# Left operands of the second MLP matmul loaded one product at a time into the shared tile pool, and every weight laid out in HBM as contiguous 512 KB blocks

## The chip, the cores and the metric

The kernel runs on one core of a Trainium2 chip. The metric is device microseconds from start to end of one execution. Engines are named as in the profile: PE (TensorE matmul), PEld (its weight load), DVE (VectorE), ACT (ScalarE), POOL (GpSimd), SP (SyncE, which here issues nearly all loads). "SPq" is SP's instruction queue. Each engine works through its own instructions in order, so a waiting instruction holds everything behind it on the same engine.

## The reference

One encoder layer in float32 for 512 tokens and a model width of 2048: neighbourhood attention, then a squared-ReLU MLP.

```
x = x + neighbourhood_attention(rms_norm(x, norm_mix), w_qkv, q_gain, k_gain, rel_bias, w_o)
a = relu(rms_norm(x, norm_mlp) @ w1)        # 512 x 2048 @ 2048 x 8192
x = x + (a * a) @ w2                        # 512 x 8192 @ 8192 x 2048
```

The change touches how weights reach the chip (all of them) and how `a * a`, written to HBM by the first MLP matmul, comes back as the left operand of the second.

## The kernel before, in words

**Precision.** Every float32 operand is split into a high part `h` (rounded to fp32r by ACT) and a low part `l` (the rest, by DVE). A product takes three matmuls: high x high, high x low, low x high.

**Stages.** First the units `v`, `q`, `k` (attention, heads run beside them), then `o`, all through `multiply` (L304). Then the MLP: eight units `h0` to `h7` for `w1` and eight units `y0_0` to `y3_1` for `w2` (block c of 2048 hidden columns, half p of the output), all objects of class `Pair` and run by `multiply_pair` (L250).

**A pair.** A pair multiplies 512 tokens by a 2048 x 1024 piece of a weight with seven products instead of eight (a Strassen-Winograd scheme). Products m = 1, 5, 6, 4 (`FIRST`) run for b = 0 to 3, then m = 2, 3, 7 (`SECOND`) for b = 0 to 3. One (m, b) is a *chunk*: one 256 x 512 weight quarter (512 KB) and 12 matmuls of 512 columns; a pair has 28 chunks, 336 matmuls. The right operands of products 5, 6, 4 and 7 are sums of quarters, built in a chain: DVE adds the raw quarter to the previous one (L219, four of seven chunks). Then ACT makes `wh` (L235) and DVE `wl` (L237).

**Pools and queue order.** Raw weights lie in the pool `raw`: ten buffers of 512 KB. `load_raw` (L189) issues the load of a chunk on SP six chunks or more ahead; it starts when a buffer of `raw` comes free, which is when DVE's `wl` of an older chunk is done. The split parts `wh`, `wl` have three buffers each. Nearly everything else (left operands, outputs on their way, temporaries) lies in the pool `tiles`, 70 buffers of 256 KB. A scheduler sets each engine's order at build time; the program does not reorder at run time.

**From h to y.** After a pair `h`, the squared result is transposed in *windows* (L702) and stored to HBM tensors `z_t` by POOL (L712, L713, L723): the four blocks and three sums of them that seven products need. Left operands of block c of the second matmul are loaded during the last pair that uses the block before (h7, y0_1, y1_1, y2_1; a *handover pair* below). `pass_on` (L753) does this: per b two loads after product 1 (`xa`, `xb`: products 5, 6 and 4, 1) and two after product 2 (`xa`: product 2; `xb`: products 3, 7), all into buffers of `raw`, that is four of its buffers per b. After product 4 (and 7) `split_left` splits them into high and low parts `a_z` (L556 on ACT, L558 on DVE) in `tiles`.

**Results.** The output of each pair y0 to y2 is added into HBM by POOL: eight accumulating DMAs of 256 KB (L750), all in the last chunks of the pair and just after. The pairs y3 load these sums (`ys`, L734), add, and store.

Of the kernel before, what the change touches and what calls it, by code (L numbers as in the profile page):

```python
# [44 lines left out]
class Unit:  # L45
# [4 lines left out]


    def __init__(self, name, src, act, done, kind):
        self.name, self.src, self.act, self.done, self.kind = name, src, act, done, kind
        self.n = KT // 4 if kind == "narrow" else KT
        self.raw, self.parts, self.ps = {}, {}, None
        self.load, self.before, self.after, self.lag = None, None, None, 0


class Pair:
# [27 lines left out]
    def quarter(self, m, b):  # L87
        r, c = self.QUARTER[m]
        r, c = self.row + (4 * b + 2 * r) * P, self.col + c * T
        return self.w[r:r + 2 * P, c:c + T].rearrange("(k p) n -> p k n", p=P)  # L90


@with_exitstack
def natten_mlp_kernel(ctx, tc, x_t, gains, w_qkv, bias, w_o, w1, w2, out_t):
    nc = tc.nc
# [75 lines left out]
    def later(lag, fn):  # L171
        side.append((pos[0] + lag, fn))
# [16 lines left out]
    def load_raw(u, i):  # L189
        if isinstance(u, Pair):  # L190
            t = u.raw[i] = raw.tile([P, 2, T], F32, tag="raw", name=f"w_{u.name}_{i[0]}")
            nc.sync.dma_start(out=t, in_=u.quarter(*i))
            return
        if i % 2:
            return
        t = raw.tile([P, 2, T], F32, tag="raw", name=f"w_{u.name}_{i}")
        if u.load is not None and i == 0:
            for m in range(2):
                nc.sync.dma_start(out=t[:, m], in_=u.src[m * P:(m + 1) * P])
                u.load(m)  # L200
# [552 lines left out]
    def pass_on(dst, block):  # L753

        loaded = {}

        loads = {1: ((T + HALF, 5, 6), (HALF, 4, 1)), 2: ((0, 2), (5 * HALF, 3, 7))}

        def split_left(b, stage):
            for (c, *ms), t in zip(loads[stage], loaded.pop((b, stage))):  # L760
                for i, m in enumerate(ms):
                    yield from parts_of(dst[b], m, t[:, :, i * HALF:(i + 1) * HALF], f"a{m}_z{block}_{b}")

        def after(m, b):
            if m in (1, 2):
                ts = []
                for i, (c, *ms) in enumerate(loads[m]):
                    t = two(f"{'xb' if i else 'xa'}_z{block}_{b}_{m}")
                    n = len(ms) * HALF
                    nc.sync.dma_start(out=t[:, :, :n],  # L770
                                      in_=z_t[4 * block + b][:, c:c + n].rearrange("(k p) n -> p k n", p=P))
                    ts.append(t)
                loaded[b, m] = ts
# [78 lines left out]
```

## Time and profile before

| | |
|---|---|
| median of 3 runs | 2107.44 us (2104.9 to 2107.91) |
| the profiled execution | 2108.97 us |
| its span, first to last instruction | 2107.2 us |
| PE busy, PEld busy | 2055.6 us (98%), 1691.3 us (80%) |
| DVE busy, ACT busy | 1546.3 us (73%), 1043.6 us (50%) |
| data moved by DMA | 400 MB, mean 190 GB/s |

A busy PE counts a matmul from start to modelled end, and matmuls overlap in the pipeline: one of 512 columns is listed with 0.39 us and the next starts 0.23 us later. So time that PE loses is read best from starts: how long a pair takes against 336 steps. The clock column is the granted TensorE clock as a share of full speed. A DMA's landing time runs from its issue on the queue to its completion.

### The profile page before, as it was taken

The numbers are of one execution on the slowest core, as the hardware profiler recorded it, in microseconds if no ns is written. First come the engines' busy times: TensorE is split into PE (matmuls) and PEld (weight loads), VectorE is DVE, ScalarE is ACT, GpSimd is POOL, SyncE is SP. The second block draws the span as 40 slices with busy tenths as digits, with TensorE's granted clock in tenths as the row PEclk, the third lists the DMA queues.
The fourth block names the chain that finished last, engine by engine and source line by source line (L and its number), as shares of the span: only waits on it lengthen the run. The fifth ranks groups of instructions, "written<-read, shape, count | busy, mean of one in ns | idle before, by whom it ended". The sixth has DMA issues, their size and how long they took to land.

```text
span 2107.2 us, 25091 instructions
## 1 busy us (share of the span) xinstructions
PE 2055.6 (98%) x9330; PEld 1691.3 (80%) x9330; DVE 1546.3 (73%) x1884; ACT 1043.6 (50%) x1412; POOL 103.7 (5%) x166
## 2 busy tenths in 40 slices
PE   9999999999999999999999999999998999989998
PEld 7888888888888887888888888887877777777777
DVE  6674774764774568778878877898797687779786
ACT  6663653654663444444544544564453445345333
POOL 0000000000000000010010110110201001011000
PEclk9999999999999999999999999999999999999999
DMA  9333333323233346676866866887888689589774
GB/s 285 100 91 90 97 90 94 96 85 101 94 100 130 102 151 217 180 223 185 276 217 205 272 209 210 289 275 256 257 305 246 193 255 274 197 239 273 257 234 147
DMA packets 251931, 400.14 MB, mean 190 GB/s; under 512 B 14240, under 2 KB 83872, under 8 KB 251808
## 3 DMA queue, kind: packets, MB, share of 16 engines
q1 hardware_dynamic: 234768, 352.37, 52.5%
q0 software_dynamic: 16896, 46.15, 7.7%
q8 instruction: 73, 1.20, 0.2%
q14 instruction: 50, 0.41, 0.1%
q10 hardware_dynamic: 144, 0.02, 0.0%
HBM read 348.14 MB, written 50.33 MB: 189 GB/s over the span
## 4 chain that ended last, share of the span: by engine, by line
PE 40%; issue 36%; DMA 12%; DVE 8%; POOL 3%; ACT 0%; SPq 0%; DVEq 0%; POOLq 0%; ACTq 0%
DMA w_y<-in_w 11%; PE mm_q L304 8%; PE mm_k L304 8%; PE mm_v L304 8%; PE mm_o L304 5%; DVE wl_y L237 4%; DVE w_y L219 2%; PE y_y L250 2%; PE x_y L250 2%; PE z_y L250 2%; PE w_y L250 1%; PE o L471 1%; POOL z L712 1%; POOL z L713 1%; POOL z L723 1%
## 5 line engine op out<-in xcount | busy, mean ns | idle before, releaser
L235 ACT ACTIVATE wh_y<-w_y 128x1024 fp32r<-128x1024 f32 x224 | 237.6, 1061 | 327.9 <-PE y_y L250 91.5
L235 ACT ACTIVATE wh_h<-w_h 128x1024 fp32r<-128x1024 f32 x224 | 237.6, 1061 | 287.0 <-PE y_h L250 85.5
L237 DVE TENSOR_TENSOR wl_h<-w_h,wh_h 128x1024 fp32r<-128x1024 f32 x224 | 272.7, 1221 | 73.9 <-ACT wh_h L235 73.4
L237 DVE TENSOR_TENSOR wl_y<-w_y,wh_y 128x1024 fp32r<-128x1024 f32 x224 | 270.8, 1219 | 24.4 <-ACT wh_y L235 24.3
L219 DVE TENSOR_TENSOR w_y<-w_y,w_y 128x1024 f32<-128x1024 f32 x128 | 156.4, 1222 | 112.5 <-DMA w_y<-in_w 110.9
L219 DVE TENSOR_TENSOR w_h<-w_h,w_h 128x1024 f32<-128x1024 f32 x128 | 155.2, 1220 | 50.9 <-DMA w_h<-in_w 50.6
L237 DVE TENSOR_TENSOR wl_o<-w_o,wh_o 128x1024 fp32r<-128x1024 f32 x32 | 39.1, 1223 | 58.5 <-ACT wh_o L235 58.4
L235 ACT ACTIVATE wh_o<-w_o 128x1024 fp32r<-128x1024 f32 x32 | 33.9, 1060 | 80.0 <-PE mm_o L304 66.2
L235 ACT ACTIVATE wh_q<-w_q 128x1024 fp32r<-128x1024 f32 x32 | 34.0, 1062 | 77.8 <-PE mm_q L304 30.2
L237 DVE TENSOR_TENSOR wl_q<-w_q,wh_q 128x1024 fp32r<-128x1024 f32 x32 | 39.2, 1226 | 43.6 <-ACT wh_q L235 42.1
L237 DVE TENSOR_TENSOR wl_k<-w_k,wh_k 128x1024 fp32r<-128x1024 f32 x32 | 39.1, 1223 | 37.8 <-ACT wh_k L235 37.8
L235 ACT ACTIVATE wh_k<-w_k 128x1024 fp32r<-128x1024 f32 x32 | 34.0, 1062 | 50.7 <-PE mm_q L304 31.1
L235 ACT ACTIVATE wh_v<-w_v 128x1024 fp32r<-128x1024 f32 x31 | 32.8, 1058 | 47.4 <-PE mm_v L304 23.4
L237 DVE TENSOR_TENSOR wl_v<-w_v,wh_v 128x1024 fp32r<-128x1024 f32 x31 | 37.9, 1224 | 23.0 <-ACT wh_v L235 22.6
L713 POOL DMA_DIRECT2D z<-zt x32 | 17.3, 542 | 467.3 <-ACT zt L708 467.0
L602 POOL DMA_DIRECT2D y<-x1t_0s x4 | 2.3, 586 | 770.9 <-ACT x1t_0s L601 770.9
L708 ACT ACTIVATE zt<-zt 128x512 f32<-128x512 f32 x64 | 37.1, 579 | 2.0 <-DVE a_z_1l L558 2.0
L511 ACT ACTIVATE t<-t,st 128x256 f32<-128x256 f32 x64 | 32.0, 501 | 10.6 <-DVE st L507 10.6
L250 PE MATMUL x_y<-wl_y,a_z_0h 128*128 128x512 f32 x64 | 26.2, 409 | 9.8 <-DVE wl_y L237 9.8
L250 PE MATMUL z_y<-wl_y,a_z_1h 128*128 128x512 f32 x64 | 25.4, 396 | 5.1 <-DVE wl_y L237 5.1
L250 PE MATMUL z_y<-wl_y,a_z_0h 128*128 128x512 f32 x64 | 26.4, 412 | 3.9 <-DVE wl_y L237 3.9
L250 PE MATMUL y_y<-wl_y,a_z_1h 128*128 128x512 f32 x64 | 25.8, 404 | 4.0 <-DVE wl_y L237 3.9
(1443 smaller groups left out, 6293.1 us busy)
## 6 DMA issues: line engine op xcount, KB each, us to landing
w_h<-in_w SPq DMA_DIRECT2D x224, 512.0 KB, 4.5
w_y<-in_w SPq DMA_DIRECT2D x224, 512.0 KB, 5.4
w_q<-in_w_qkv SPq DMA_DIRECT2D x32, 512.0 KB, 3.8
w_k<-in_w_qkv SPq DMA_DIRECT2D x32, 512.0 KB, 3.9
w_o<-in_w_o SPq DMA_DIRECT2D x32, 512.0 KB, 3.7
xb_z<-z SPq DMA_DIRECT2D x32, 512.0 KB, 5.0
w_v<-in_w_qkv SPq DMA_DIRECT2D x31, 512.0 KB, 3.8
z<-zt POOLq DMA_DIRECT2D x32, 256.0 KB, 4.1
```

What stands on the lines that cost most here:

```text
L219: nc.vector.tensor_tensor(out=s, in0=s, in1=u.raw[u.CHAIN[m], b], op=ALU.add)
L235: kept(nc.scalar.activation(h, s, AF.Copy))
L237: kept(nc.vector.tensor_tensor(out=l, in0=s, in1=h.bitcast(F32), op=ALU.subtract))
L250: nc.tensor.matmul(out=u.banks[x][j], lhsT=a[:, c], rhs=w[:, k], start=(m in u.FIRST and b + k + n == 0), stop=(b == NB - 1 and k == 1 and ...
L304: nc.tensor.matmul(out=ps, lhsT=a, rhs=b, start=(k == 0 and m == 0), stop=(k == KT - 1 and m == 2))
L471: nc.tensor.matmul(out=dst, lhsT=a, rhs=b, start=(n + m == 0), stop=(n == 3 and m == 2), skip_group_check=True)
L511: nc.scalar.activation(halves[i], halves[i], AF.Exp, bias=st[:, i:i + 1], accum_out=st[:, 2 + i:3 + i])
L602: nc.gpsimd.dma_start(out=dst, in_=t)
L708: nc.scalar.activation(t[:, i], ps, AF.Square)
L712: nc.gpsimd.dma_start(out=dst[:, :T], in_=t[:, 1])
L713: nc.gpsimd.dma_start(out=dst[:, T:T + HALF], in_=t[:, 0, :HALF])
L723: nc.gpsimd.dma_start(out=dst[:, T + HALF:].rearrange("p (k n) -> p k n", k=2), in_=s)
```

## The change

Two things are changed.

*Weights.* The host rearranges all weights. Each load of two 128-row pieces by 512 columns (or eight by 128 columns for `q` and `k`) becomes one contiguous block of 512 KB in HBM, 4 KB for each of the 128 partitions. Before, a load of `v`, `o`, `w1` or `w2` read 256 pieces of 2 KB, one of `q` or `k` 1024 pieces of 512 bytes. Number, size, order and buffers of these loads stay. (The very first one stays in two halves of 2 KB per partition.)

*Left operands.* `z_t` gets the layout [partition, product, k, 256]; one product of one b is 2 KB in a row per partition. `pass_on` now loads one product (256 KB) after each chunk, seven loads per b in place of four, into a buffer `zr` of `tiles` instead of `raw`, and splits it six steps (two chunks) later. The bytes are the same. The stores of `z_t` now write pieces of 1 KB: 256 for L712's, 128 for L713's, 512 for L723's.

```diff
     def quarter(self, m, b):
         r, c = self.QUARTER[m]
         r, c = self.row + (4 * b + 2 * r) * P, self.col + c * T
-        return self.w[r:r + 2 * P, c:c + T].rearrange("(k p) n -> p k n", p=P)
+        return self.w[r // (2 * P), c // T]
...
-        elif u.kind != "narrow":
-            nc.sync.dma_start(out=t, in_=u.src[i * P:(i + 2) * P].rearrange("(k p) n -> p k n", p=P))
         else:
-            nc.sync.dma_start(out=t.rearrange("p a (k n) -> p (a k) n", n=P),
-                              in_=u.src[i * T:(i + 2) * T].rearrange("(k p) n -> p k n", p=P))
+            nc.sync.dma_start(out=t, in_=u.src(i))
...
-    z_t = [dram.tile([2 * P, 7 * HALF], F32, name=f"z_{i}", tag=f"z_{i}") for i in range(2 * FP)]
+    z_t = [dram.tile([P, 7, 2, HALF], F32, name=f"z_{i}", tag=f"z_{i}") for i in range(2 * FP)]
...
-            t, dst = lefts[name], z_t[2 * p + half][k * P:(k + 1) * P]
+            t, dst = lefts[name], z_t[2 * p + half][:, :, k]
...
-                nc.gpsimd.dma_start(out=dst[:, :T], in_=t[:, 1])
-                nc.gpsimd.dma_start(out=dst[:, T:T + HALF], in_=t[:, 0, :HALF])
+                nc.gpsimd.dma_start(out=dst[:, 0:2], in_=t[:, 1].rearrange("p (m n) -> p m n", m=2))
+                nc.gpsimd.dma_start(out=dst[:, 2], in_=t[:, 0, :HALF])
...
-                nc.gpsimd.dma_start(out=dst[:, T + HALF:].rearrange("p (k n) -> p k n", k=2), in_=s)
+                nc.gpsimd.dma_start(out=dst[:, 3:7], in_=s.rearrange("p a (m n) -> p (a m) n", m=2))
...
+        order = (2, 4, 1, 5, 6, 3, 7)
         loaded = {}
 
-        loads = {1: ((T + HALF, 5, 6), (HALF, 4, 1)), 2: ((0, 2), (5 * HALF, 3, 7))}
-
-        def split_left(b, stage):
-            for (c, *ms), t in zip(loads[stage], loaded.pop((b, stage))):
-                for i, m in enumerate(ms):
-                    yield from parts_of(dst[b], m, t[:, :, i * HALF:(i + 1) * HALF], f"a{m}_z{block}_{b}")
+        def load(m, b):
+            t = loaded[m, b] = wtile(f"zr{m}_z{block}_{b}")
+            nc.sync.dma_start(out=t.rearrange("p (k n) -> p k n", k=2), in_=z_t[4 * block + b][:, order.index(m)])
+
+        def split_left(m, b):
+            yield from parts_of(dst[b], m, loaded.pop((m, b)).rearrange("p (k n) -> p k n", k=2), f"a{m}_z{block}_{b}")
 
         def after(m, b):
-            if m in (1, 2):
...
-            elif m in (4, 7):
-                start(split_left(b, 1 if m == 4 else 2))
+            load(m, b)
+            later(6 * STEP, lambda: start(split_left(m, b)))
         return after
...
+    def blocks(w):
+        return w.reshape(-1, 2, P, w.shape[1] // T, T).transpose(0, 3, 2, 1, 4)
+
+    def narrow(w):
+        return w.reshape(-1, 8, P, w.shape[1] // P, P).transpose(0, 3, 2, 1, 4).reshape(2, -1, P, 2, T)
```

Up to the end of pair h6 the order of instructions on every engine is as before; it differs from h7 on. In the names below `w_y1_1_4` is the raw quarter for product 4 of pair y1_1, and `zr5_z2_0` the left operand of product 5, block 2, b = 0; the last number is a running one.

SP at the start of the handover pair y1_1, before:

```order
L192 DMA w_y1_1_5_13705<-in_w2 128x2x512
L192 DMA w_y1_1_6_13730<-in_w2 128x2x512
L770 DMA xa_z2_0_1_13755<-z_8_133 128x2x512
L770 DMA xb_z2_0_1_13757<-z_8_133 128x2x512
L192 DMA w_y1_1_4_13759<-in_w2 128x2x512
L192 DMA w_y1_1_1_13779<-in_w2 128x2x512
```

The same place now:

```order
L193 DMA w_y1_1_5_13753<-in_w2 128x1024
L193 DMA w_y1_1_6_13778<-in_w2 128x1024
L193 DMA w_y1_1_4_13805<-in_w2 128x1024
L193 DMA w_y1_1_1_13827<-in_w2 128x1024
L193 DMA w_y1_1_5_13854<-in_w2 128x1024
L759 DMA zr1_z2_0_13803<-z_8_133 128x512
L759 DMA zr5_z2_0_13825<-z_8_133 128x512
L193 DMA w_y1_1_6_13881<-in_w2 128x1024
```

Three weight loads have moved ahead of the first left operand, and what stands between weights is 256 KB at a time instead of two times 512 KB.

DVE early in y1_0, around the add that is the third row from below, before:

```order
L237 TENSOR_TENSOR wl_y1_0_6_13264<-w_y1_0_6_13161,wh_y1_0_6_13263 128x1024
L219 TENSOR_TENSOR w_y1_0_5_13236<-w_y1_0_5_13236,w_y1_0_1_13215 128x1024
L219 TENSOR_TENSOR w_y1_0_5_13313<-w_y1_0_5_13313,w_y1_0_1_13294 128x1024
L237 TENSOR_TENSOR wl_y1_0_4_13282<-w_y1_0_4_13194,wh_y1_0_4_13281 128x1024
L219 TENSOR_TENSOR w_y1_0_6_13257<-w_y1_0_6_13257,w_y1_0_5_13236 128x1024
```

And now:

```order
L217 TENSOR_TENSOR w_y1_0_6_13305<-w_y1_0_6_13305,w_y1_0_5_13284 128x1024
L217 TENSOR_TENSOR w_y1_0_5_13361<-w_y1_0_5_13361,w_y1_0_1_13342 128x1024
L235 TENSOR_TENSOR wl_y1_0_6_13312<-w_y1_0_6_13210,wh_y1_0_6_13311 128x1024
L217 TENSOR_TENSOR w_y1_0_4_13324<-w_y1_0_4_13324,w_y1_0_6_13305 128x1024
L235 TENSOR_TENSOR wl_y1_0_4_13330<-w_y1_0_4_13239,wh_y1_0_4_13329 128x1024
```

The add of the quarter for product 5 of a far later chunk (`..._13313`, now `..._13361`) still stands ahead of the `wl` that PE needs next, and one `wl` earlier than before.

SP in the second half of h7, before:

```order
L192 DMA w_h7_2_11427<-in_w1 128x2x512
L770 DMA xa_z0_0_2_11457<-z_0_125 128x2x256
L770 DMA xb_z0_0_2_11459<-z_0_125 128x2x512
L192 DMA w_h7_3_11464<-in_w1 128x2x512
L192 DMA w_h7_7_11493<-in_w1 128x2x512
```

The same place now:

```order
L193 DMA w_h7_3_11479<-in_w1 128x1024
L759 DMA zr1_z0_3_11362<-z_3_128 128x512
L759 DMA zr5_z0_3_11390<-z_3_128 128x512
L759 DMA zr6_z0_3_11418<-z_3_128 128x512
L759 DMA zr4_z0_3_11446<-z_3_128 128x512
L759 DMA zr2_z0_0_11477<-z_0_125 128x512
L193 DMA w_h7_7_11509<-in_w1 128x1024
```

Five left operands now stand in a row between two weight loads; each waits for a buffer of `tiles`, several of them for PE to be done with an older operand.

## Rows read from the trace of the kernel before

**Rows 1.** Windows: attention and o; all y pairs (columns: next group)

```profile
60.00:778.00 718.00, 717.91 (x3434) 601.45 (x3433) 443.12 (x663) 370.61 (x609) 6.70 (x12) 1.00 0.33 101
...
1426.30:2107.20 680.90, 636.40 (x2721) 513.25 (x2719) 535.60 (x572) 304.31 (x352) 48.71 (x60) 0.98 0.77 240
```

**Rows 2.** Windows of single pairs: h6, then y0_0 to y3_1 in order

```profile
core 0: us, PE busy (x) PEld busy (x) DVE busy (x) ACT busy (x) POOL busy (x), PEclk, DMA share, GB/s
...
1265.50:1345.50 80.00, 80.00 (x369) 66.17 (x368) 65.56 (x74) 39.53 (x46) 6.49 (x12) 1.00 0.72 234
...
1426.30:1510.30 84.00, 80.99 (x370) 66.01 (x369) 71.21 (x82) 41.76 (x50) 9.39 (x16) 1.00 0.72 246
1510.30:1593.60 83.30, 78.79 (x338) 63.85 (x336) 68.86 (x77) 45.33 (x58) 5.89 (x7) 0.98 0.92 289
1593.60:1681.20 87.60, 81.18 (x338) 64.92 (x337) 65.31 (x65) 33.46 (x35) 8.79 (x10) 0.96 0.71 213
1681.20:1766.10 84.90, 79.04 (x337) 63.80 (x336) 68.06 (x75) 44.97 (x57) 5.27 (x6) 0.98 0.87 261
1766.10:1854.10 88.00, 80.07 (x337) 64.66 (x336) 65.31 (x65) 33.45 (x35) 8.79 (x10) 0.96 0.71 213
1854.10:1937.60 83.50, 78.83 (x337) 63.89 (x336) 68.98 (x76) 44.77 (x57) 5.27 (x6) 0.98 0.90 272
1937.60:2022.00 84.40, 79.40 (x338) 63.76 (x337) 69.92 (x75) 31.86 (x32) 5.30 (x6) 0.98 0.78 241
2022.00:2107.20 85.20, 78.09 (x337) 62.38 (x335) 57.95 (x62) 28.70 (x28) 0.00 (x0) 0.99 0.54 186
```

**Rows 3.** Timeline of PE in y1_0: start us, us, instruction, idle before

```profile
1611.05 0.39 PE L250 MATMUL x_y<-wh_y,a_z_1h 128*128 128x512 f32 x1
...
1617.17 0.39 PE L250 MATMUL w_y<-wh_y,a_z_1h 128*128 128x512 f32 x1
1620.48 0.50 PE L250 MATMUL w_y<-wl_y,a_z_1h 128*128 128x512 f32 x1 [2.93 <-DVE wl_y L237]
...
1623.13 0.63 PE L250 MATMUL w_y<-wh_y,a_z_1h 128*128 128x512 f32 x1
1623.55 0.63 PE L250 MATMUL w_y<-wl_y,a_z_1h 128*128 128x512 f32 x1
```

**Rows 4.** Timeline of PE: the last matmul

```profile
2100.99 0.39 PE L250 MATMUL y_y<-wh_y,a_z_3l 128*128 128x512 f32 x1
```

**Rows 5.** Waits of the whole span: us in total, times, longest us

```profile
DVE w_y L219 <- DMA w_y<-in_w: 110.9, 54, 5.9
```

**Rows 6.** Timeline of DVE in y1_0: start us, us, instruction, idle before

```profile
1618.07 1.23 DVE L219 TENSOR_TENSOR w_y<-w_y,w_y 128x1024 f32<-128x1024 f32 x1 [5.18 <-DMA w_y<-in_w]
```

**Rows 7.** Tile w_y: landing after issue, in 1596 to 1613 and 1640 to 1656

```profile
DMA to landing us min/median/max: 5.8/11.1/12.2
DMA to landing us min/median/max: 3.4/4.7/5.3
```

**Rows 8.** DMA queues, 1600 to 1616 us: packets, MB, share of 16 engines

```profile
q0 software_dynamic: 864, 1.57, 58.5%
q1 hardware_dynamic: 1445, 2.78, 48.8%
```

**Rows 9.** The same of 1640 to 1670, and of 60 to 150 us

```profile
q1 hardware_dynamic: 3013, 5.81, 57.9%
...
q1 hardware_dynamic: 9976, 8.89, 33.2%
```

**Rows 10.** DMA issues: queue, count, KB each, median us from issue to landing

```profile
z<-zt_0s POOLq DMA_DIRECT2D x16, 512.0 KB, 5.6
...
xa_z<-z SPq DMA_DIRECT2D x16, 512.0 KB, 5.1
...
xa_z<-z SPq DMA_DIRECT2D x16, 256.0 KB, 5.3
```

**Rows 11.** Line 723, the store of sums: duration ns min/median/max, first and last start

```profile
L723 POOL DMA_DIRECT2D z<-zt_0s x16: 539/539/539, 919.1 to 1496.5; - x16
```

More of the change, by code (lines that the diff above doesn't have):

```diff
@@ L89, in quarter, with natten_mlp_kernel @@
         r, c = self.row + (4 * b + 2 * r) * P, self.col + c * T
-        return self.w[r:r + 2 * P, c:c + T].rearrange("(k p) n -> p k n", p=P)
+        return self.w[r // (2 * P), c // T]
 @with_exitstack
-def natten_mlp_kernel(ctx, tc, x_t, gains, w_qkv, bias, w_o, w1, w2, out_t):
+def natten_mlp_kernel(ctx, tc, x_t, gains, w_qk, w_v, bias, w_o, w1, w2, out_t):
     nc = tc.nc
@@ L198, in load_raw @@
             for m in range(2):
-                nc.sync.dma_start(out=t[:, m], in_=u.src[m * P:(m + 1) * P])
+                nc.sync.dma_start(out=t[:, m], in_=u.src(0)[:, m])
                 u.load(m)
-        elif u.kind != "narrow":
-            nc.sync.dma_start(out=t, in_=u.src[i * P:(i + 2) * P].rearrange("(k p) n -> p k n", p=P))
-        else:
-            nc.sync.dma_start(out=t.rearrange("p a (k n) -> p (a k) n", n=P),
-                              in_=u.src[i * T:(i + 2) * T].rearrange("(k p) n -> p k n", p=P))
+        else:
+            nc.sync.dma_start(out=t, in_=u.src(i))
         if u.load is not None and i:
@@ L523, in natten_mlp_kernel @@
     for g in range(NG):
-        u = Unit(f"v{g}", w_qkv[:, 2 * D + g * T:2 * D + (g + 1) * T], xa, v_done(g), "tokens")
+        u = Unit(f"v{g}", lambda i, g=g: w_v[i // 2, g], xa, v_done(g), "tokens")
         units.append(u)
@@ L527, in natten_mlp_kernel @@
             hd = Head(h)
-            units.append(Unit(f"q{h}", w_qkv[:, h * P:(h + 1) * P], xa, run_on(hd.query), "narrow"))
-            units.append(Unit(f"k{h}", w_qkv[:, D + h * P:D + (h + 1) * P], xa, run_on(hd.attend), "narrow"))
+            units.append(Unit(f"q{h}", lambda i, h=h: w_qk[i // 2, h], xa, run_on(hd.query), "narrow"))
+            units.append(Unit(f"k{h}", lambda i, h=h: w_qk[i // 2, HEADS + h], xa, run_on(hd.attend), "narrow"))
     def enter_ahead(i):
@@ L658, in natten_mlp_kernel @@
     for g in range(NG):
-        u = Unit(f"o{g}", w_o[:, g * T:(g + 1) * T], oa, o_done(g), "wide")
+        u = Unit(f"o{g}", lambda i, g=g: w_o[i // 2, g], oa, o_done(g), "wide")
         u.before = load_residual(g)
@@ L753, in pass_on @@
     def pass_on(dst, block):
+        order = (2, 4, 1, 5, 6, 3, 7)
         loaded = {}
-        loads = {1: ((T + HALF, 5, 6), (HALF, 4, 1)), 2: ((0, 2), (5 * HALF, 3, 7))}
-        def split_left(b, stage):
-            for (c, *ms), t in zip(loads[stage], loaded.pop((b, stage))):
-                for i, m in enumerate(ms):
-                    yield from parts_of(dst[b], m, t[:, :, i * HALF:(i + 1) * HALF], f"a{m}_z{block}_{b}")
-        def after(m, b):
-            if m in (1, 2):
[L766 to L773, printed above, removed]
-            elif m in (4, 7):
-                start(split_left(b, 1 if m == 4 else 2))
+        def load(m, b):
[3 more added lines that the diff above has]
+            yield from parts_of(dst[b], m, loaded.pop((m, b)).rearrange("p (k n) -> p k n", k=2), f"a{m}_z{block}_{b}")
+        def after(m, b):
+            load(m, b)
+            later(6 * STEP, lambda: start(split_left(m, b)))
         return after
@@ L833 @@
                                  a["na_q_gain"].reshape(1, P), a["na_k_gain"].reshape(1, P)]).T,
-        "w_qkv": a["na_w_qkv"][0],
+        "w_qk": narrow(a["na_w_qkv"][0][:, :2 * D]),
+        "w_v": blocks(a["na_w_qkv"][0][:, 2 * D:]),
         "bias": bias,
-        "w_o": a["na_w_o"][0],
-        "w1": a["mlp_w1"][0],
-        "w2": a["mlp_w2"][0],
+        "w_o": blocks(a["na_w_o"][0]),
+        "w1": blocks(a["mlp_w1"][0]),
+        "w2": blocks(a["mlp_w2"][0]),
     }
```

## Prediction

> **What bounds the kernel now.** I read the windows by stage first [rows 1]: PE is busy 717.9 of 718 us in attention and `o`, and 636.4 of 680.9 in the `y` pairs; between them a late `h` pair, h6, has it busy for all of its 80.0 us [rows 2]. The reader is to see that the stages before 1426 us leave nothing to gain (h0 waits for a norm that the change doesn't touch), and that all the change can win lies in the `y` pairs.
>
> Next I priced a pair. In an unhindered stretch 27 matmul starts take 1617.17 - 1611.05 = 6.12 us [rows 3], 0.2267 us each, so 336 take 76.2 us. A pair with windows takes 80.0 (h6, where PE is never idle [rows 2]). Against these, from the lengths in [rows 2]: y0_0 loses 4.0 (it has windows too), y0_1 7.1, y1_0 11.4, y1_1 8.7, y2_0 11.8, y2_1 7.3, y3_0 8.2, y3_1 9.0. Of the last, 6.0 is the end of the kernel: the last matmul starts at 2100.99 [rows 4], the span ends at 2107.2, and one step of 0.2 is work. So the eight `y` pairs lose 67.5 - 6.0 = 61.5 us to waits.
>
> What waits is to be seen at one place. PE starts the high half of a chunk at 1617.17 and its `wl` matmul only at 1620.48, after 2.93 us of idling for DVE; then it steps at 0.42 us instead of 0.23 [rows 3], the lower of its two clock levels (1.2 instead of 2.4 GHz), and the granted clock of the pair falls to 0.96 [rows 2]. So a stall of 3 us costs about half as much again. DVE itself had stood idle for 5.18 us until 1618.07, for a raw weight to land [rows 6]. That add belongs to a much later chunk; it only stands ahead of the needed `wl` in DVE's order. Over the whole span such adds in the `y` pairs wait 110.9 us in 54 cases [rows 5]. PE sees what is longer than its cover: here 5.18 - 2.93 = 2.25 us.
>
> Why does the weight land late? Around 1600 us a weight lands 11.1 us after its issue; forty us later, with nothing else in flight, 4.7 us [rows 7]. In 1600 to 1616 the accumulating stores (q0) take 58.5% of the DMA engines' time for 1.57 MB while the loads get 48.8% [rows 8]: the DMA is full.
>
> **The change part by part.**
>
> *Contiguous weights, q, k, v, o, h.* PE is full there [rows 1, 2], so shorter loads are hidden behind its work; worth 0, and if that cover were gone they would still gain, not cost. *In the y pairs* a cheaper load counts, since the DMA is full in places. No row shows a 4 KB piece. Pieces of 2 KB run at 5.81 MB in 57.9% of 30 us, 334 GB/s; the stretch of mostly 512-byte pieces at 8.89 MB in 33.2% of 90 us, 298 GB/s [rows 9]. A fixed cost per piece fitted to these two speeds gives 341 GB/s for 4 KB, 2% better; the bounds are 0 and the 12% that the step from 512 bytes brought. I take 2%, since the fixed part has mostly been spread by 2 KB. A weight block is 0.524 MB or 1.57 us of all engines per chunk, so this is 28 x 0.03 = 0.9 us of DMA time in a pair, and at most 5.
>
> *Left operands out of `raw`.* Ten `raw` buffers are ten chunks of lookahead; per b, four of them went to `xa` and `xb`. Without these the lookahead in a handover pair, and in the pair after it, stays near ten. Also the weights no longer queue behind 1 MB at a time (two times 0.524 MB at 334 GB/s is 3.1 us) but behind 256 KB (0.8 us). What is left is what the DMA must move. A handover pair needs 28 x (0.524 + 0.262) = 22.0 MB of loads, 65.9 us at 334 GB/s, and about eight accumulating stores of the pair before: 16 x 0.585 = 9.4 us for 1.57 MB [rows 8], so 12.5 us for 2.1 MB. That is 78.4 us; measured shares say 76.6, 73.9 and 75.2 (0.92 x 83.3, 0.87 x 84.9, 0.90 x 83.5 [rows 2]). Against 76.2 us of PE this is a second bound: y0_1, y1_1 and y2_1 will not get clean. Of their 7.1, 8.7 and 7.3 us I leave 4.5 each, between 2 (spread evenly, with the 0.9 off) and 7 (nothing helps). Gain 9.6.
>
> *The pairs after a handover.* y1_0, y2_0 and y3_0 lose most (31.4 together) though they load no left operands of their own. Their start meets two things: the accumulating stores, and SP catching up on weights that had no `raw` buffer before. The first stays: in those 16 us weights need 1.57/2.72 = 58% beside 58.5%, 16% too much, so 16 x 0.16 = 2.6 us of lateness. The second goes. A landing of 4.7 + 2.6 = 7.3 instead of about 11 takes some 4 us off DVE's wait of 5.18, below the cover of 2.25: PE sees nothing at that place. I leave 2.0 each, below the 3.0 that y3_1 loses with neither in front of it but with loads of sums inside; bounds 0 and 8. Gain 25.4. y0_0, which follows h7: 4.0 to 2.5, gain 1.5. y3_1 stays at 3.0.
>
> *The new loads' own waits.* A `zr` is gated by a `tiles` buffer and read by ACT about two to three chunks later (by the waits in the program), 5.4 to 8.2 us, against 5.3 us for a landing of 256 KB [rows 10]: hidden, except beside the accumulating stores, and in the second half of h7, where five stand in a row on SP ahead of a weight and ACT comes to them almost at once. Behind a waiting ACT stands the next `wh`, and then PE. I take 1.0 us for h7 (bounds 0 and 6).
>
> *Stores of `z_t`.* The POOL instruction of L723 takes 0.539 us [rows 11], now for 512 pieces instead of at most 256; bounds: unchanged, or in proportion, 2.2 us. Its landing, 5.6 us [rows 10], moves as much; its `raw` buffers come free later, and weights of the next `h` pair queue behind. h6 loses nothing now, so some of it is covered: 0.5 us in all, between 0 and 8.
>
> Forty-eight more loads cost SP a few tenths of a us each, on an engine that only issues.
>
> A rule of the Trainium skill speaks against the change: the page "DMA: Bandwidth & Descriptors", section "Rules for kernel authors", says to coalesce small transfers into large ones, and its section on the anatomy of a DMA gives about 2 us fixed per transfer. By its figure 48 more transfers would be an estimated 96 us of fixed cost. Whether that is paid or overlapped is the fourth rival.
>
> Sum: 9.6 + 25.4 + 1.5 - 1.0 - 0.5 = 35.0 us. The profiled execution took 2108.97, 1.5 above the median of the runs, so 2108.97 - 35.0 = 2074.
>
> **Rivals.**
>
> 1. *The adds keep their place, so lookahead buys little.* DVE's order still puts an add ahead of a needed `wl`, a `wl` earlier even than before, two chunks after its load is released; a landing above some 7 us then stalls DVE whatever the lookahead. For it: the add rows in the change; against it: half the load in front of those weights is gone. Then the pairs after a handover keep two thirds of 31.4, a gain of 10 instead of 25: 2090; with handover pairs unchanged 2099.
>
> 2. *Everything clears.* If landings near 5 us return everywhere, 61.5 - 3.0 = 58.5 goes: 2050. Against it: the 75 to 78 us of DMA work in a pair of 76.2. For it: the first `y` pair's quiet part and `h` pairs lose nothing at DMA shares of 0.7.
>
> 3. *Slower: the stores in 1 KB pieces hold `raw` buffers.* Place: start of h2 to h7 and y0_0, where weights wait for buffers of stored sums. Price: to undo the 35 and be 0.2% slower, seven pairs must lose (35 + 4)/7 = 5.6 us each, which with the low clock (half as much again) is 3.7 us of stall beyond the cover; it decides from stores that land about 4 us later than now, and L723 in proportion gives 1.7. At 6.5 us a pair: 2074 + 45 = 2119. Against it: h6's loss of 0.
>
> 4. *Slower: transfers cost by number.* 256 KB lands after 5.3 us and 512 KB after 5.1 [rows 10], so the time seems to go by the piece; 48 more at 5.2 us would be 250 us if each held the queue: 2320. Against it: in 1640 to 1670, 5.81 MB [rows 9] is a block every 2.7 us while each lands after 4.7 [rows 7]: they overlap. By this the rule named above does not apply, and the trace disagrees with paying it.
>
> 5. *No effect*: the accumulating stores alone set all waits; 2106.
>
> **How the numbers follow.** Forecast 2074 (2060 to 2088): 0.54. Rival 1: 0.19. Rival 2: 0.13. No effect: 0.06. Rival 3: 0.06, rival 4: 0.02. The range 2056 to 2099 holds the forecast, most of rival 1 and half of rival 2, some 0.8. About 0.2% is what a measurement of this kernel can tell from no change. Faster by more than that: 0.54 + 0.19 + 0.13 = 0.86; same 0.06; slower 0.08.
>
> **What would show it.** Right: y1_0, y2_0 and y3_0 near 78 us, handover pairs near 81, the clock column back near 1.00, the waits of the `w_y` adds for DMA well below half of 110.9, and landings of weights at a pair's start near 7 us. Rival 1: those waits stay above 80 us and the stall of `w_y` some 24 us into y1_0 is still there. Rival 3: `h` pairs above 80.5 us, and L723 well above 0.54 us. Wrong altogether: PE waiting behind ACT for `zr`, or DMA shares in the handover pairs that fall while PE still loses.

## The result, and the profile after

The changed kernel takes 2083.14 us (median of 4 runs, 2081.29 to 2085.78), the kernel before, run beside it, 2107.68: a ratio of 0.9868, 95% interval 0.9849 to 0.9886. That is 24.5 us less. The prediction said 2074 with a range of 2056 to 2099, so the time lies inside it. The pairs show that it got there by another way.

The windows of single pairs after, in order h0, h6, y0_0 to y3_1 (columns as in [rows 2], whose lines they answer):

```profile
778.10:858.30 80.20, 79.03 (x359) 65.13 (x358) 69.92 (x76) 44.98 (x57) 2.16 (x4) 1.00 0.60 202
1258.50:1338.60 80.10, 80.10 (x370) 66.19 (x370) 63.63 (x72) 39.63 (x46) 8.15 (x12) 1.00 0.69 230
1419.60:1502.20 82.60, 81.13 (x370) 65.90 (x370) 69.34 (x80) 40.81 (x49) 11.29 (x16) 1.00 0.72 245
1502.20:1587.90 85.70, 78.88 (x338) 64.43 (x337) 74.53 (x84) 45.86 (x58) 5.62 (x7) 0.96 0.92 295
1587.90:1667.70 79.80, 77.34 (x337) 62.61 (x336) 60.60 (x60) 33.18 (x34) 7.74 (x10) 1.00 0.71 212
1667.70:1753.50 85.80, 80.20 (x337) 64.43 (x336) 72.25 (x80) 45.74 (x58) 6.23 (x8) 0.96 0.89 278
1753.50:1834.10 80.60, 77.73 (x338) 62.80 (x338) 61.40 (x61) 32.86 (x35) 8.05 (x10) 1.00 0.72 214
1834.10:1918.60 84.50, 79.57 (x338) 63.73 (x337) 72.17 (x80) 45.90 (x58) 5.92 (x7) 0.98 0.91 281
1918.60:1997.20 78.60, 77.06 (x338) 62.88 (x337) 66.62 (x70) 31.93 (x33) 5.24 (x6) 1.00 0.80 251
1997.20:2079.50 82.30, 76.47 (x337) 62.70 (x335) 57.74 (x61) 28.70 (x28) 0.00 (x0) 0.98 0.54 188
```

The span shrank by 27.7 us (2107.2 to 2079.5). By pairs, before minus after: y1_0, y2_0 and y3_0 gained 7.8, 7.5 and 5.8 (together 21.0), y0_0 1.4, y3_1 2.9. The handover pairs y0_1, y1_1 and y2_1 became longer by 2.4, 0.9 and 1.0. And h0, of which the prediction said that it leaves nothing to gain, gained 5.4; the rest is 0.8 ahead of it and small change in h2 and h7. What PE itself waits in the `y` pairs fell from 38.4 us, all of it for DVE's `wl`, to 25.3; 5.6 of these are a wait for ACT.

The waits of the whole span after (us in total, times, longest us; the first line answers [rows 5]):

```profile
DVE w_y L217 <- DMA w_y<-in_w: 68.1, 38, 5.4
...
ACT a_z_0h L554 <- DMA zr_z<-z: 48.5, 17, 11.0
...
ACT a_z_3h L554 <- DMA zr_z<-z: 29.6, 16, 4.9
```

DVE's waits at the adds fell from 110.9 to 68.1 us. ACT's waits for left operands grew, from some 28 us (`xa` and `xb`, the longest 6.6) to 108 (`zr`). Behind the longest of them, in y0_1, PE stood too: ACT first, then PE (start us, us, instruction, idle before in brackets):

```profile
1522.60 0.63 ACT L554 ACTIVATE a_z_0h<-zr_z 128x512 fp32r<-128x512 f32 x1 [10.99 <-DMA zr_z<-z]
1523.14 1.04 ACT L233 ACTIVATE wh_y<-w_y 128x1024 fp32r<-128x1024 f32 x1
```

```profile
1524.23 0.80 PE L248 MATMUL y_y<-wh_y,a_z_1h 128*128 128x512 f32 x1 [5.57 <-ACT wh_y L233]
```

What the stall at the start of the other two handover pairs looks like is seen in y1_1: PE, then DVE, then ACT:

```profile
1670.43 0.39 PE L248 MATMUL z_y<-wh_y,a_z_0h 128*128 128x512 f32 x1
1675.03 0.79 PE L248 MATMUL z_y<-wl_y,a_z_0h 128*128 128x512 f32 x1 [4.21 <-DVE wl_y L235]
```

```profile
1672.62 1.23 DVE L217 TENSOR_TENSOR w_y<-w_y,w_y 128x1024 f32<-128x1024 f32 x1 [5.38 <-DMA w_y<-in_w]
1673.76 1.22 DVE L235 TENSOR_TENSOR wl_y<-w_y,wh_y 128x1024 fp32r<-128x1024 f32 x1
```

```profile
1673.97 0.63 ACT L554 ACTIVATE a_z_0h<-zr_z 128x512 fp32r<-128x512 f32 x1 [7.71 <-DMA zr_z<-z]
```

PE has the high half of the second chunk and waits 4.21 us for its `wl`. DVE makes that `wl` at 1673.76, but idled 5.38 us in front of the add just ahead of it. This is the picture of [rows 3, 6], in another pair. ACT idles beside it for a left operand until 1673.97. Which of these waits matters, and what the two parts of the change have to do with them, is what the experiments tell.

### The profile page after: what moved, and what is told of

Same layout as the page of the kernel before. It is cut to its first block, busy times and chain, and to the rows that moved or that the text cites. A ratio compares the mean times of both kernels' runs of the same rounds, so it can differ in the third digit from the quotient of the medians.

```text
span 2079.5 us, 25226 instructions
## 1 busy us (share of the span) xinstructions
PE 2044.1 (98%) x9330; PEld 1684.3 (81%) x9330; DVE 1546.5 (74%) x1884; ACT 1045.5 (50%) x1412; POOL 116.7 (6%) x166
## 5 line engine op out<-in xcount | busy, mean ns | idle before, releaser
L235 DVE TENSOR_TENSOR wl_h<-w_h,wh_h 128x1024 fp32r<-128x1024 f32 x224 | 272.8, 1221 | 77.4 <-ACT wh_h L233 76.7
L235 DVE TENSOR_TENSOR wl_y<-w_y,wh_y 128x1024 fp32r<-128x1024 f32 x224 | 271.0, 1219 | 24.5 <-ACT wh_y L233 24.0
L217 DVE TENSOR_TENSOR w_y<-w_y,w_y 128x1024 f32<-128x1024 f32 x128 | 156.1, 1220 | 70.9 <-DMA w_y<-in_w 68.1
L233 ACT ACTIVATE wh_q<-w_q 128x1024 fp32r<-128x1024 f32 x32 | 34.0, 1062 | 77.8 <-PE mm_q L302 30.2
L233 ACT ACTIVATE wh_k<-w_k 128x1024 fp32r<-128x1024 f32 x32 | 34.0, 1062 | 50.8 <-PE mm_q L302 31.1
L554 ACT ACTIVATE a_z_0h<-zr_z 128x512 fp32r<-128x512 f32 x28 | 17.6, 627 | 50.4 <-DMA zr_z<-z 48.5
L554 ACT ACTIVATE a_z_3h<-zr_z 128x512 fp32r<-128x512 f32 x28 | 17.5, 626 | 29.6 <-DMA zr_z<-z 29.6
```

The source lines that it names most:

```text
L217: nc.vector.tensor_tensor(out=s, in0=s, in1=u.raw[u.CHAIN[m], b], op=ALU.add)
L233: kept(nc.scalar.activation(h, s, AF.Copy))
L235: kept(nc.vector.tensor_tensor(out=l, in0=s, in1=h.bitcast(F32), op=ALU.subtract))
L554: nc.scalar.activation(view(h), src, AF.Copy)
```

## The experiments

Ratios are to the kernel before, run on the same chip (2108 to 2114 us there). Each pair length below is of one execution. Two kernels whose DVE, ACT, SP, POOL and PE orders are the same row for row (the changed kernel and `add_later`, below) differ by up to 1.1 us in a pair and by 0.0004 in the ratio, so one pair tells some 1 us, no less. Pair h0 tells less still: the changed kernel and `later24` (below), which are the same up to h7, have 80.2 and 82.7 there.

| kernel | ratio (95%) | h0 | y0_1 | y1_0 | y1_1 | y2_0 | y2_1 | y3_0 | y3_1 |
|---|---|---|---|---|---|---|---|---|---|
| before | 1 | 85.6 | 83.3 | 87.6 | 85.0 | 88.0 | 83.5 | 84.4 | 85.2 |
| changed | 0.9868 (0.9849 to 0.9886) | 80.2 | 85.7 | 79.8 | 85.8 | 80.5 | 84.5 | 78.6 | 82.4 |
| weights_only | 0.9883 (0.9855 to 0.9910) | 81.4 | 81.2 | 83.6 | 82.1 | 82.3 | 82.6 | 82.5 | 85.1 |
| left_only | 0.9997 (0.9985 to 1.0009) | 82.9 | 88.3 | 86.7 | 86.4 | 86.5 | 88.8 | 82.9 | 86.2 |
| blocks_2k | 0.9931 (0.9913 to 0.9950) | 84.8 | 86.7 | 82.8 | 84.2 | 85.8 | 85.3 | 83.2 | 83.4 |
| far_4k | 0.9860 (0.9840 to 0.9879) | 80.6 | 85.6 | 80.2 | 85.5 | 80.1 | 87.0 | 79.0 | 83.4 |
| plain_store | 0.9736 (0.9710 to 0.9762) | 80.8 | 79.9 | 76.2 | 78.2 | 77.4 | 80.3 | 77.3 | 82.3 |
| left_plain | 0.9870 (0.9854 to 0.9886) | 83.1 | 82.6 | 80.5 | 83.2 | 80.1 | 83.9 | 79.2 | 86.5 |
| later24 | 0.9822 (0.9798 to 0.9846) | 82.7 | 84.8 | 76.6 | 85.3 | 76.6 | 85.0 | 77.1 | 83.1 |
| add_later | 0.9864 (0.9844 to 0.9883) | 80.9 | 86.2 | 80.9 | 85.3 | 81.2 | 83.5 | 79.7 | 83.5 |
| add_later24 | 0.9810 (0.9780 to 0.9840) | 81.3 | 84.8 | 76.5 | 85.5 | 77.0 | 83.5 | 76.2 | 84.4 |
| presum | 0.9839 (0.9814 to 0.9863) | 81.9 | 82.2 | 82.1 | 79.3 | 82.0 | 81.5 | 81.1 | 82.7 |
| all3 | 0.9712 (0.9692 to 0.9732) | 80.3 | 78.2 | 76.8 | 77.5 | 76.8 | 77.6 | 76.8 | 83.2 |
| pinned_add | 0.9677 (0.9661 to 0.9693) | 80.9 | 76.2 | 77.0 | 76.2 | 77.0 | 76.2 | 77.0 | 82.4 |

### The two parts apart

`weights_only` is the kernel before with this alone:

```diff
-        return self.w[r:r + 2 * P, c:c + T].rearrange("(k p) n -> p k n", p=P)
+        return self.w[r // (2 * P), c // T]
```

(and the same for the other units and the host). `left_only` is the changed kernel with that undone.

> The kernel before with the weights alone laid out in 512 KB blocks; the left operands come as xa and xb as before. Theory A (each part pays where it acts: the weight layout gives what was not forecast, that is h0 85.6 to 80.2 us, y3_1 85.2 to 82.4, the start 0.8 and h2 0.7, while the pairs after a handover are won by the left operands): about 2098 us, h0 near 80.2, y1_0 and y2_0 still above 86. Theory B (shorter weight loads also win the pairs after a handover): about 2085, y1_0 and y2_0 near 80. Theory C (as forecast, the layout is worth next to nothing): 2105, h0 still 85.6.

> The changed kernel with the weights laid out as before (pieces of 2 KB, and of 512 bytes for q and k); the left operands one product at a time into the shared pool. Theory A: about 2093 us, h0 back at 85.6, y1_0 and y2_0 near 80 as in the changed kernel. Theory B (the weight layout does the work): 2100 or more, y1_0 and y2_0 at 85 or more. Theory C: 2086.

Weights alone bring 0.9883, left operands alone nothing. In the totals theory B stands, against the forecast (theory C) and against the theory formed from the two traces (A). By pairs it is B for `left_only`; y1_0 and y2_0 of `weights_only`, 83.6 and 82.3, lie between B's 80 and A's 86. The pairs from y0_1 to y2_1 of `weights_only`, with the DVE order of before:

```profile
1506.40:1587.50 81.10, 78.10 (x337) 62.31 (x336) 71.24 (x79) 44.93 (x58) 5.91 (x7) 1.00 0.94 298
1587.50:1671.10 83.60, 78.79 (x338) 64.00 (x338) 63.69 (x64) 33.45 (x35) 8.77 (x10) 0.98 0.72 222
```

and the same two of `left_only`, with the DVE order of after:

```profile
1507.40:1595.70 88.30, 79.73 (x337) 63.67 (x336) 74.91 (x83) 45.58 (x58) 6.94 (x8) 0.96 0.90 282
1595.70:1682.40 86.70, 79.57 (x338) 62.16 (x337) 62.24 (x63) 33.09 (x35) 7.67 (x10) 1.00 0.69 204
```

The new left operands move time rather than save it: against the kernel before, `left_only` loses 5.0, 1.4 and 5.3 us in the handover pairs and wins some 1 to 1.5 in each of the pairs after them. (The 2.7 less in h0, which they don't touch, is about the spread of that pair.) The layout shortens both kinds.

### What of the layout it is

The layout changes two things: pieces of 4 KB instead of 2 KB, and all pieces of a load side by side in HBM. `blocks_2k` keeps the second only, `far_4k` the first only (pieces of 4 KB lying 16 or 64 KB apart).

```diff
 blocks_2k
-        return w.reshape(-1, 2, P, w.shape[1] // T, T).transpose(0, 3, 2, 1, 4)
+        return w.reshape(-1, 2, P, w.shape[1] // T, T).transpose(0, 3, 1, 2, 4)
 far_4k
+        return w.reshape(-1, 2, P, w.shape[1] // T, T).transpose(0, 2, 3, 1, 4)
```

> The changed kernel, its weights still contiguous blocks of 512 KB in HBM, but inside a block one 128-row piece stands behind the other, so that a load of v, o, w1 or w2 again reads 256 pieces of 2 KB instead of 128 of 4 KB (q and k keep 4 KB). Theory A (the size of a piece does it: where loads and accumulating stores share the DMA engines, larger pieces get a larger share of them): like the kernel with the old weight layout, ratio to the kernel before 0.995 to 1.0. Theory B (what helps is that a block lies together in HBM): like the changed kernel, 0.985 to 0.988.

> The changed kernel, but the 4 KB of a partition no longer stand beside those of the next partition: the 128 pieces of a load of v, o, w1 or w2 lie 16 or 64 KB apart in HBM (128 pieces of 4 KB, spread). With the other three layouts (2 KB spread: ratio 0.9997 to the kernel before, 2 KB together: 0.9931, 4 KB together: 0.9868) this closes the square. Theory A (only the size of a piece counts, and the 2 KB blocks gained by the longer pieces of q and k): like 4 KB together, 0.985 to 0.989. Theory B (size and place in HBM each bring half): 0.992 to 0.995. Theory C (the place counts, the size nothing): 0.997 or more.

Pieces of 4 KB do all of it, near (0.9868) or far (0.9860). Pieces of 2 KB cost 0.9997 when spread and 0.9931 when together, about half. That `blocks_2k` fell between its two theories is not explained by its longer pieces of `q` and `k`: its h0 starts 0.7 us earlier than that of `left_only`, while its eight `y` pairs together are 15 us shorter. Why place matters to 2 KB pieces and not to 4 KB ones stays open.

What changes with it is when a load lands. In these four, which run the same orders, the mean time from issue to landing of the `y` pairs' weights (worked out from the trace, 211 to 214 loads each) is 5.88 us (2 KB, spread), 5.63 (2 KB, together), 5.41 (4 KB, spread) and 5.36 (4 KB, together), and the time falls in the same order. Half a microsecond per load goes with 27 us.

### Whether it goes through the accumulating stores

The prediction put the lateness down to the accumulating stores. `plain_store` stores plainly in the changed kernel and so leaves out the sum over the blocks, `left_plain` does so in `left_only`:

```diff
-                nc.gpsimd.dma_start(out=y_sum[c, 2 * p + half], in_=t, accum_op=ALU.add)
+                nc.gpsimd.dma_start(out=y_sum[c, 2 * p + half], in_=t)
```

> The changed kernel, but the outputs of y0 to y2 are stored plainly and not added into HBM, so the sum over the blocks is left out (the last two blocks alone reach the output). Theory A (the accumulating stores take the DMA engines at the start of a pair, so that weights and left operands land late there): landings at a pair's start fall to about 5 us, y0_1, y1_1 and y2_1 to about 81, the pairs after them by about 1, total about 2068. Theory B (the stores are no more than load among other load; ACT waits for left operands that were issued too late anyway): the handover pairs stay above 84, total 2081 or more.

> The weights laid out as before, left operands one product at a time, and the outputs of y0 to y2 stored plainly, not added into HBM (the sum over the blocks is left out: the last two blocks alone reach the output). Compared with the same plain stores and the new weight layout (2057 us). Theory A (the layout pays only beside the accumulating stores): 2063 or less, nearly all of it in h0, y0_0 and the start. Theory B (the layout makes all loads land sooner, stores or not): 2075 or more, the y pairs 2 to 4 us longer each.

The stores matter (theory A of the first, and more than it said): 1.32% with the new layout, 1.27% with the old. But the layout is worth as much without them (0.9870 to 0.9736) as with them (0.9997 to 0.9868; theory B of the second). So it does not work through the stores. Both make landings later or sooner, and the kernel pays for late landings with or without the stores. That asks why a kernel with some ten chunks of lookahead has no slack at all.

### ACT's waits for left operands

```diff
-            later(6 * STEP, lambda: start(split_left(m, b)))
+            later(24 * STEP, lambda: start(split_left(m, b)))
```

> The changed kernel, but a left operand is split 24 steps (six chunks) after its load is issued in place of 6, so that ACT comes to it some 16 us later. Theory A (in the handover pairs ACT waits for the left operand and holds the next wh behind it): ACT's waits for zr all but vanish, y0_1, y1_1 and y2_1 go from 85.7, 85.8 and 84.5 to about 82, total about 2073. Theory B (the raw weights land late beside the accumulating stores and DVE's adds wait for them, whatever ACT does): these pairs stay within 1 us, total 2082 to 2084. Theory C (six more buffers of the shared pool are held, so loads start later): slower, 2086 or more.

The total is theory A's (0.9822; its 2073 would be 0.9836), and ACT's waits for `zr` go from 108 us to 3. But the gain is not where theory A said: y0_0 goes to 80.3 and the pairs after a handover to 76.6 to 77.1, clean, and the handover pairs stay at 85, as theory B has it. Windows of y1_0 and y1_1, and DVE in y1_1:

```profile
1587.70:1664.30 76.60, 76.48 (x338) 63.01 (x337) 62.42 (x64) 35.05 (x38) 6.96 (x10) 1.00 0.75 221
1664.30:1749.50 85.20, 78.66 (x337) 63.91 (x336) 70.35 (x77) 43.22 (x54) 6.97 (x10) 0.98 0.88 282
```

```profile
1669.58 1.23 DVE L217 TENSOR_TENSOR w_y<-w_y,w_y 128x1024 f32<-128x1024 f32 x1 [5.76 <-DMA w_y<-in_w]
```

With ACT's 7.71 us gone, DVE's wait at the add is as long as before (5.76 against 5.38). In y0_1 PE's wait behind ACT is gone too, and one of 5.7 us for a `wl` behind an add, where DVE waits 7.9, stands in its place. DVE's waits at the adds are longer in all than in the changed kernel, 80.5 us against 68.1, though the time is shorter: the sum of such waits does not tell what PE pays. In the pairs after a handover the last `a_z` splits now stand among DVE's first rows of the pair. In the changed kernel DVE had run ahead into an add of y1_0:

```profile
1604.63 1.22 DVE L217 TENSOR_TENSOR w_y<-w_y,w_y 128x1024 f32<-128x1024 f32 x1 [4.00 <-DMA w_y<-in_w]
```

With later splits it has work there, and no wait of that length is left in y1_0 (the longest is 2.8 us, and PE waits for nothing in that pair).

### DVE's order

`add_later` and `add_later24` put three steps ahead of each add, and two in place of five behind it; the second has later24's edit as well.

```diff
+            yield 3 * STEP
             if m in u.CHAIN:
                 nc.vector.tensor_tensor(out=s, in0=s, in1=u.raw[u.CHAIN[m], b], op=ALU.add)
-            yield 5 * STEP
+            yield 2 * STEP
```

> The changed kernel, but every add that builds a right operand stands three steps (some 2 us) later in DVE's order, nearer to the chunk that needs it. Theory A (what PE loses is the time that DVE waits at an add for a raw weight of a later chunk, with the needed wl behind it): each long stall of the y pairs shrinks by about 2 us, the short ones vanish: about 2068, y1_0 and y2_0 below 78, the stall at the second chunk of y1_1 5 us instead of 6.7. Theory B (PE waits for something else, ACT's waits for left operands or the weights' own landing before their wl): no change, 2081 or more. Theory C (wh now waits for the add): slower, h pairs above 80.5.

> The changed kernel with both single edits together: left operands are split 24 steps after their load, and the adds of right operands stand three steps later. Alone the first left the handover pairs at 85 us (there DVE still waited 5.8 us at an add for a raw weight), the second too (there ACT still waited 5.8 us for a left operand). Theory A (two waits stand side by side and end within some 1.5 us of each other, so that taking one away shows the other): now y0_1, y1_1 and y2_1 fall to 82 to 83, total ratio 0.977 to 0.980. Theory B (neither is the cause; the raw weights themselves land after their wl is needed): these pairs stay at 85, ratio 0.982 as for the first edit alone.

Nothing changed (0.9864 and 0.9810), but these runs speak for no theory: the edit did not reach the program. The scheduler set the same rows; in `add_later` no row of any engine differs from the changed kernel, in `add_later24` seven neighbours on DVE have swapped places against `later24`. They serve as repeats. The order that it sets, DVE at the start of y1_1 in the changed kernel, shows why:

```order
L217 TENSOR_TENSOR w_y1_1_5_13854<-w_y1_1_5_13854,w_y1_1_1_13827 128x1024
L235 TENSOR_TENSOR wl_y1_1_5_13760<-w_y1_1_5_13671,wh_y1_1_5_13759 128x1024
```

The add is for product 5 of b = 2 (`..._13854`), the `wl` behind it for product 5 of b = 0, eight chunks earlier. The scheduler has floated the add up, it seems to where it takes the raw weight to have landed (what it assumes of a load is not shown here). Of the 128 adds of the `y` pairs, 34 have seven or eight other `wl` between them and their own in the order of the kernel before, and 75 in the changed kernel's. So the longer lookahead went into adds that stand still further ahead of their need, and at 38 of them DVE has to wait for the load.

`pinned_add` holds the add behind the DVE instruction written before it, on top of later24's edit:

```diff
-                nc.vector.tensor_tensor(out=s, in0=s, in1=u.raw[u.CHAIN[m], b], op=ALU.add)
+                tc.keep_in_program_order(nc.vector.tensor_tensor(out=s, in0=s, in1=u.raw[u.CHAIN[m], b], op=ALU.add))
```

> The changed kernel with left operands split 24 steps after their load, and with every add of right operands pinned behind the DVE instruction written before it in the code. In the two kernels with the add three steps later the scheduler had floated the adds back to (nearly) the same rows; pinned, the add for a chunk stands some one to three chunks ahead of that chunk in place of nine, so the wl that PE needs next no longer stands behind an add whose raw weight was just issued. Theory A (what PE loses at a pair's start is this place in DVE's order; the late landing beside the accumulating stores only sets how long): DVE's waits at the adds nearly vanish, y0_1, y1_1 and y2_1 fall from 85 to 79 or less, total ratio to the kernel before 0.970 to 0.974. Theory B (there the raw weights land after their own chunk needs them, since the accumulating stores hold the engines; only fewer bytes help): these pairs stay above 83, ratio 0.979 to 0.982. Theory C (an add so near to its chunk makes wh and wl late): slower, h pairs above 80.5, ratio above 0.984.

Theory A, and more than it said: 2044.78 us (2043.89 to 2045.22, 5 runs), 0.9677. Windows of y0_1, y1_0 and y1_1, then DVE around the second chunk of y1_1:

```profile
1500.30:1576.50 76.20, 76.20 (x338) 63.09 (x337) 70.10 (x77) 42.60 (x53) 6.68 (x8) 1.00 1.01 339
1576.50:1653.50 77.00, 76.70 (x338) 62.88 (x337) 63.78 (x65) 35.58 (x39) 7.21 (x9) 1.00 0.75 226
1653.50:1729.60 76.10, 76.10 (x337) 63.05 (x336) 70.10 (x77) 42.60 (x53) 6.65 (x8) 1.00 0.95 311
```

```profile
1657.50 2.35 DVE L235 TENSOR_TENSOR wl_y<-w_y,wh_y 128x1024 fp32r<-128x1024 f32 x2
1659.78 1.22 DVE L217 TENSOR_TENSOR w_y<-w_y,w_y 128x1024 f32<-128x1024 f32 x1
```

The handover pairs are at 76.2, the floor that the prediction priced. In DVE's order one other `wl` now stands between each add of a `y` pair and its own. Of DVE's 68.1 us of waits in this row of the whole span there is left:

```profile
DVE w_y L217 <- DMA w_y<-in_w: 1.0, 2, 0.8
```

The weights did not come sooner. Landing after issue of `w_y` at the start of y1_1, 1648 to 1662 us here and, second, 1662 to 1676 us of the changed kernel:

```profile
DMA to landing us min/median/max: 3.8/11.6/13.7
```

```profile
DMA to landing us min/median/max: 4.5/6.4/11.3
```

They land later than in the changed kernel, with the same accumulating stores beside them, and cost nothing; over the loads of all `y` pairs the mean is 5.74 us, against 5.50 in `later24` and 5.36 in the changed kernel. In the handover pairs this settles the cause: a landing was paid for because of the place of the add in DVE's order. (There PE's order is that of `later24` row for row, and ACT's and SP's rows move by at most two and four places. In h0, y0_0 and the pairs after a handover the pin moves rows of PE too, by up to 22 places, so there it is not the add alone.) This kernel is faster than both. Two things were not run: the pin in the kernel before, and the old layout beside the pin, which would tell whether the layout still pays.

### Sums without accumulating stores

`presum` lets every `y` pair load the running sum after its product 4, as y3 does, lets DVE add it, and stores plainly; `all3` adds the edits of `add_later24`.

```diff
-                if last:
+                if held:
                     nc.vector.tensor_tensor(out=add, in0=add, in1=ys[c, half], op=ALU.add)
...
-                nc.gpsimd.dma_start(out=y_sum[c, 2 * p + half], in_=t, accum_op=ALU.add)
+                nc.gpsimd.dma_start(out=y_sum[c, 2 * p + half], in_=t)
...
-            u.prefetch = prefetch if c == NCH - 1 else None
+            u.prefetch = prefetch
```

> The changed kernel, but every y pair loads the running sum of its output after its product 4 (as y3 does), DVE adds it, and POOL stores the result plainly: no accumulating stores, 256 KB loads in quiet chunks instead. Theory A (the accumulating stores, which hold the DMA engines about 176 ns per 2 KB piece, make the starts late): y1_1 and y2_1 near 80, total 2060 to 2070. Theory B (the sums only move: 16 more loads per two pairs, DVE's extra adds and the eight extra buffers of the shared pool give it back): 2080 or more.

> Both edits of the run before, and no accumulating stores (every y pair loads the running sum and DVE adds it). Theory A (the stores, ACT's waits and DVE's adds are separate parts of the same stalls): 0.970 to 0.975, the y pairs near 79. Theory B (the loads of sums and the buffers they hold cost what the rest brings): 0.980 or more.

`presum` helps the handover pairs; the pairs after them become 1.5 to 2.5 us longer: 0.9839, between its theories, and its interval overlaps that of the changed kernel. `all3` is 0.9712, theory A, though in effect it is `presum` with later splits, since the adds stay where the scheduler floats them. Leaving out the accumulating stores is the second way out, hardly behind the first (the intervals touch): it takes lateness away where `pinned_add` makes it harmless.

## Why the prediction was right, and for which wrong reasons

**What bounds the kernel.** The stall was read rightly: an add for a far later chunk ahead of the needed `wl`. The step that the stages before the `y` pairs leave nothing to gain was wrong for h0. There PE waited for the norm of the MLP, which DVE made late, since it had stood at the same kind of add. The window of h0, DVE and PE before, then PE after:

```profile
778.90:864.50 85.60, 81.77 (x358) 67.25 (x357) 69.67 (x75) 45.06 (x57) 2.17 (x4) 0.96 0.63 188
```

```profile
835.55 1.23 DVE L219 TENSOR_TENSOR w_h<-w_h,w_h 128x1024 f32<-128x1024 f32 x1 [3.00 <-DMA w_h<-in_w]
```

```profile
840.83 1.12 PE L654 MATMUL r_a<-ident,an 128*128 128x128 f32 x4 [3.83 <-DVE an L365]
```

```profile
837.33 0.66 PE L652 MATMUL r_a<-ident,an 128*128 128x128 f32 x4 [1.17 <-DVE an L363]
```

In the four kernels with 2 KB pieces h0 takes 82.9 to 85.6 us, in the ten with 4 KB 80.2 to 82.7; by the means (84.1 and 81.1) the layout is worth some 3 us there, and the rest of the 5.4 is within the spread of that pair. A full PE up to 778 us, from a window that ended there, says nothing of the pair that begins there.

**Contiguous weights: the term that failed.** It was set at 0 in `h` and at 0.9 us of DMA time in a pair, and entered the sum nowhere. Measured: 25 us alone (0.9883) and 27 us on top of the new left operands (0.9997 to 0.9868). The price of a 4 KB piece was not far off: the median transfer record is 84 ns for 2 KB and 159 for 4 KB, 5% less per byte, within the bounds of 0 to 12%. What failed is turning it into time by the engines' load. The wait at an add ends when one load lands, so the landing of that load counts, whatever the engines' mean load is.

**Left operands out of `raw`.** This carried 36.5 of the forecast 35.0 us. Measured: nothing alone (0.9997), and 0.9883 to 0.9868 on top of the layout, 3 us with overlapping intervals. Longer lookahead bought nothing, since the adds moved ahead with it in DVE's order (75 of 128 far ahead in place of 34). That is rival 1's mechanism; it was right, and its signs half: the `w_y` waits are at 68.1 us, below its 80, but by the layout, since `left_only` has 88.3; and the stall 24 us into y1_0 is gone (PE's longest wait in that pair is 2.1 us). Its price of 2090 is 7 us from the result, the forecast 9.

**The second bound.** The handover pairs were said not to get clean, for 78.4 us of DMA work against 76.2 of PE. In `pinned_add` y0_1 takes 76.2 with a DMA share of 1.01 and 339 GB/s: the engines are full and PE loses nothing. The gain of 9.6 us there was a loss of 4.3. At 0.9677 that kernel is past rival 2's 2050 (0.973), and not by rival 2's condition, landings near 5 us everywhere.

**The pairs after a handover.** Forecast 25.4 us and y0_0 1.5; measured 21.0 and 1.4, by the layout and the left operands together. The number is near, the reason is not the one given: in these three pairs the layout alone brings 11.6 us (`weights_only`), the left operands alone 3.9 (`left_only`).

**The new loads' own waits.** 1.0 us was set for h7, where 0.3 was lost. That they wait beside the accumulating stores was said and not priced: there ACT waits for `zr` up to 11.0 us, and in y0_1 PE stood 5.57 us behind it, which the prediction had named as the sign of being wrong altogether. What these waits cost is not shown. The 10 us of `later24` (0.9868 to 0.9822) came in y0_0 and the pairs after a handover, where the edit gave DVE other work ahead of the adds, and in y0_1 a stall as long took the place of ACT's.

**Stores of `z_t`.** The instruction that [rows 11] showed at 539 ns:

```profile
L721 POOL DMA_DIRECT2D z<-zt_0s x16: 752/779/788, 912.8 to 1488.5; - x16
```

779 ns for at least twice the pieces, between the bounds (the upper one, 2.2 us, took four times the pieces; twice would be 1.1); the landing is 5.6 us as before. The `h` pairs after h0 stay at 80.05: the cost is 0 in place of 0.5, and rival 3 falls.

**Transfers by number.** `pinned_add` issues all of the 48 added transfers and has the handover pairs at the floor: they overlap, and rival 4 falls. The rule of the Trainium skill named there ("DMA: Bandwidth & Descriptors", section "Rules for kernel authors": coalesce) sets no time here by their number. Another row of that section says to issue a DMA early and to wait on its semaphore late. The runs agree: the kernels before and after issued early and waited early, and waiting late is what `pinned_add` adds, where landings of 11.6 us (median at the start of y1_1) cost nothing. The 2 us behind the prediction's 96 stand, on that page of the Trainium skill, for DMAs that GpSimd issues; these loads are SP's.

So two errors met: a term of 36.5 that was worth 3 or nothing, and one near 0 that was worth some 25. That the total lies 9 us from the forecast is luck; the range held since it reached to rival 1.

## What to carry to other kernels

Before costing a faster load, find what waits for its landing, and where that instruction stands in its engine's order: an instruction that stands far ahead of its need turns the lateness of its load into a stall of everything behind it, and a deeper prefetch does not help where the instruction moves ahead with it. Pin it near its use first; here that, on top of the later splits, took the handover pairs to the floor, with later landings. Test a two-part change by its parts even when the total came out as forecast, and see in the built order that an edit reached the program before reading its time.

## What the runs showed of the hardware

- The median records of hardware-queue pieces are 27, 46, 84 and 159 ns for 512 bytes, 1, 2 and 4 KB (the first three of the kernel before, the last of the changed one). 9 ns per piece and 37.5 ns per KB give 28, 47, 84 and 159. The two figures of the line are an estimate fitted to these four medians. An accumulating 2 KB piece has 176 ns in the same traces, twice the 84.
- Pieces of 2 KB land sooner when the load's pieces lie side by side (mean 5.63 us in `blocks_2k` against 5.88 in `left_only`), which goes with 0.66% of the time here; for pieces of 4 KB (5.36 and 5.41 us) no difference in time was seen. The cause is open.
- 16 DMA engines full for a whole pair (share 1.01, 339 GB/s) did not slow PE, DVE or ACT: y0_1 of `pinned_add` runs at a granted clock of 1.00 and at the floor, and its `wl` and `wh` take 1221 and 1062 ns on DVE and ACT, as in y2_0 of that kernel at a share of 0.75 (1221 and 1063).
